# The value half of the first memory's projection computed inside the first cross attention

## The chip, the cores and the metric

One core of a Trainium2 chip runs the whole program. The metric is the device time of one execution in microseconds; the kernel before takes 2530.24 us, the median of three runs (2525.29 to 2534.04). Five engines work beside each other, each with its own queue of instructions in a fixed order: TensorE (PE, with its weight loads shown as PEld), VectorE (DVE), ScalarE (ACT), GpSimd (POOL) and SyncE (SP), which issues most DMAs.

## The reference

Two blocks of layers act on 256 tokens of width 1024. The first block has two layers; each mixes the tokens, then attends to a memory of 256 rows, then applies a feed-forward. The change concerns the first layer: its mixing (a recurrence over time, RWKV, beside a state space part, S5) and the cross attention that follows it:

```python
h = h + y_mix
y_mem = memory_cross_attention(rms_norm(h, norm_xattn), rms_norm(mem, norm_mem), w_q, w_kv, ...)

def memory_cross_attention(h, mem_n, w_q, w_kv, q_gain, k_gain, w_o):
    q = rms_norm((h @ w_q).reshape(b, t, 4, 256), q_gain)
    k, v = split(mem_n @ w_kv, 2)            # w_kv: 1024 x 2048
    k = rms_norm(k.reshape(b, m, 4, 256), k_gain)
    p = softmax(einsum('bthd,bmhd->bhtm', q, k) / 16)
    return einsum('bhtm,bmhd->bthd', p, v) @ w_o
```

The keys and values depend on the memory and the weights alone, and not on the tokens, so they can be computed at any time before they are used. All arithmetic is in 32-bit floats.

## The kernel before

A product with a weight matrix is done in three matmuls. `wt` (L250) loads a weight tile in two halves of 512 KB (128 x 1024 floats) on SP's queue into `raw` buffers; ACT casts each half to a rounded `whi` (L270), DVE subtracts to get the rest `wlo` (L271). `mm3` then multiplies high by high (L320), high by low and low by high (L321, L322). The activations are split in the same way into `xTh` and `xTl` when a norm transposes them (`norm_part`, L379: transposes at L385 on PE, casts at L361 on ACT, subtractions at L362 on DVE, squares at L401 on ACT).

The work is written in phases. `mix0` is the first mixing layer, `xa0` the first cross attention, `ff0` the feed-forward after it. Weight buffers belong to a pool `wp` that is opened anew when a phase wants other sizes: in `mix0` there are 3 raw and 2 split buffers, from `xa0` on 6 and 6 (L47, L48).

Within a phase, pieces of work are Python generators. `drive` (L280) takes one step of each in turn, then one step of a background generator; this order of writing is the priority from which a planner fixes each engine's order when the program is built, by its own costs. In the recurrence, background steps are also tied to stand behind the last matmul of the recurrence written before them (`pace`).

`mem_kv` (L500) computes keys and values of one memory. Its first step loads the memory (two tiles of 512 KB, L506), normalizes it, and allocates `kT` and `v`. Then come four chunks of 512 columns, chunks 0 and 1 keys, 2 and 3 values. A chunk takes two weight tiles (four loads of 512 KB) and eight steps of six matmuls, `psA` group D being its place in PSUM. A key chunk is normalized and transposed afterwards; a value chunk is copied out of PSUM with a scale (L544).

In `mix0` this generator is the background of the recurrence: `rwkv` (L1022) runs `mat` (L1178) for four pairs of heads, two at a time, beside S5 (`s5_main`, L1466, whose scans and products run on DVE and POOL), and takes a step of `mem_kv` per round (L1322). Within `mat`, five rounds of small matmuls (L1225, L1238 to L1241) alternate with a product on DVE (Y, L1227) and a copy on ACT (TZ, L1243); L1248 closes them. After it follow the gate matrix (`s5_glu`) and the output projection.

`xattn` (L576) works on two halves of heads, `attn(0)` and `attn(1)`. Each projects its queries with `w_q` in eight steps of six matmuls (`proj_M`), normalizes and transposes them, and for two blocks of tokens forms scores (L601), softmax and transposed probabilities (L620, L621). Then the product with `v` (L628) and its split follow. The second half starts eight rounds after the first (XI), so its projection lies beside the first half's softmax. `out_proj` with `w_o` is written behind both, and the planner lays its first half beside the second half's softmax. The PSUM group of the query projections alternates between A and D; the product with `v` of the first half uses A (XP).

Of the kernel before, what the change touches and what calls it, by code (L numbers as in the profile page):

```python
# [9 lines left out]
F32 = mybir.dt.float32  # L10
# [22 lines left out]
GC = 3  # L33
RB = 2
XI, XP = 8, ('A', None)
KV_ORD = ((0, 1, 2, 3), (0, 2, 1, 3))
R0 = 2
R1 = 2
# [166 lines left out]
def build(tc, dram, off, out, phases):  # L205
# [7 lines left out]
    ap = None  # L213
# [97 lines left out]
    def idle(n):  # L311
        for _ in range(n):
            yield

    def chain(*fns):
        for f in fns:
            yield from f
# [177 lines left out]
            down_acc(y, lambda k: xh[:, k], lambda k: xl[:, k], name, i, order[0], -1)  # L495
        down_last(y, lambda k: xh[:, k], lambda k: xl[:, k], name, order[last:])

    mem_state, mem_pools, mem_ctx = {}, {}, {}

    def mem_kv(l, tag, st, xp=None):  # L500
        m = [wp.tile([128, 1024], F32, tag="raw", name="mem", bufs=nraw) for _ in range(2)] if rawc == 1024 else None
        if m is None:
            m2 = wp.tile([128, 2, 1024], F32, tag="raw", name="mem", bufs=nraw)
            m = [m2[:, t] for t in range(2)]
        for t in range(2):
            nc.sync.dma_start(m[t], dram("mem")[:, t])  # L506
        xh, xl, rm = norm_T(m, "norm_mem%d" % l, tag, xp)
        gk = ap.tile([128, 2], F32, tag="gk", name="gk", bufs=1)
        V.scalar_tensor_tensor(gk, colr("xa_q_gain%d" % l), 1.0 / 16.0, colr("xa_k_gain%d" % l),
                               op0=ALU.mult, op1=ALU.mult)  # L510
        p = mem_pools[l]
        kT, v = p.tile([128, 8, 256], F32, name="kT"), p.tile([128, 2, 1024], F32, name="v")
        mem_state[l] = (kT, v)
        yield
        def heads_T(c, kn, ks):
            for t in range(2):
                for a in range(2):
                    s = slice(a * 256, a * 256 + 256)
                    V.tensor_scalar(kn[t][:, s], kn[t][:, s], ks[t][:, a:a + 1], None, op0=ALU.mult)
                pt = psC((128, 4, 128))  # L520
                for b in range(4):
                    T.transpose(pt[:, b], kn[t][:, b * 128:(b + 1) * 128], ident)
                for b in range(2):
                    S.activation(kT[:, 4 * c + b:4 * c + 4:2, t * 128:t * 128 + 128], pt[:, b::2], AF.Copy,
                                 scale=gk[:, b:b + 1])

        pend = None
        for c in KV_ORD[l]:
            ps = [psA(tag=tag) for _ in range(2)]
            for j in range(2):  # L530
                w = wt("w_kv%d" % l, 2 * c + j)
                for kk in range(4):
                    k = 4 * j + kk
                    for t in range(2):
                        ts = slice(t * 128, t * 128 + 128)
                        wh, wl = w(kk * 512, 512)
                        mm3(ps[t], xh[:, k, ts], xl[:, k, ts], wh, wl, k == 0, k == 7)
                    yield
                if pend:
                    heads_T(*pend)  # L540
                    pend = None
            if c >= 2:
                for t in range(2):
                    S.activation(v[:, t, (c - 2) * 512:(c - 1) * 512], ps[t], AF.Copy, scale=rm[t])  # L544
                continue
            kn = [st.tile([128, 512], F32, tag="kn", name="kn", bufs=2) for _ in range(2)]
            for t in range(2):
                S.copy(kn[t], ps[t])
            pend = (c, kn, head_norm(kn, rm, 2, 256, st))
        if pend:  # L550
            heads_T(*pend)

    def open_kv(l):
        mem_ctx[l] = ExitStack()
        mem_pools[l] = mem_ctx[l].enter_context(
            tc.tile_pool(name="kv%d" % l, bufs=1, side="right", reuse_waits="tile"))

    def head_norm(src, rm, nh, d, st=None):
        ss = ap.tile([128, 2, nh], F32, tag="hn%d" % nh, name="hn", bufs=2)
# [13 lines left out]
        z = rms_fold(ss, nh, d, EPS, rm)  # L573
        return [z[:, t] for t in range(2)]

    def xattn(l):  # L576
        kT, v = mem_state[l]
        xh, xl, rm = norm_T(ht, "norm_xattn%d" % l)
        oh = ap.tile([128, 8, 256], F32R, tag="oTh", name="oTh", bufs=1)
        ol = ap.tile([128, 8, 256], F32R, tag="oTl", name="oTl", bufs=1)  # L580
        def attn(c):
            ps = yield from proj_M(xh, xl, "w_q%d" % l, c)
            q = ap.tile([128, 2, 512], F32, tag="q", name="q", bufs=2)
            for t in range(2):
                S.copy(q[:, t], ps[t])
            rq = head_norm([q[:, t] for t in range(2)], rm, 2, 256)
            qT = ap.tile([128, 4, 256], F32, tag="qT", name="qT", bufs=2)
            for b2 in range(2):
                pt = psC((128, 2, 2, 128))
                for a in range(2):  # L590
                    for t in range(2):
                        b = 2 * b2 + a
                        T.transpose(pt[:, a, t], q[:, t, b * 128:(b + 1) * 128], ident)
                S.copy(qT[:, 2 * b2:2 * b2 + 2].rearrange("p a t -> p (a t)"), pt.rearrange("p a t c -> p (a t c)"))
            yield
            pT = ap.tile([128, 2, 2, 256], F32, tag="pT", name="pT", bufs=2)
            for t in range(2):
                sc = psB((128, 2, 256))
                for a in range(2):
                    for d in range(2):  # L600
                        T.matmul(sc[:, a], qT[:, 2 * a + d, t * 128:(t + 1) * 128], kT[:, 4 * c + 2 * a + d],  # L601
                                 start=d == 0, stop=d == 1)
                nm = ap.tile([128, 2], F32, tag="nm", name="nm", bufs=2)
                V.tensor_reduce(nm, sc, axis=AX, op=ALU.max, negate=True)
                nb = ap.tile([128, 2], F32, tag="nb", name="nb", bufs=2)
                V.tensor_tensor(nb, nm, rq[t], op=ALU.mult)
                p = ap.tile([128, 2, 256], F32, tag="p", name="p", bufs=2)
                sm = ap.tile([128, 2], F32, tag="sm", name="sm", bufs=2)
                for a in range(2):
                    S.activation(p[:, a], sc[:, a], AF.Exp, bias=nb[:, a:a + 1], scale=rq[t][:, a:a + 1],  # L610
                                 accum_out=sm[:, a:a + 1])
                rc = ap.tile([128, 2], F32, tag="rc", name="rc", bufs=2)
                V.reciprocal(rc, sm)
                for a in range(2):
                    V.tensor_scalar(p[:, a], p[:, a], rc[:, a:a + 1], None, op0=ALU.mult)
                yield
                pt = psC((128, 2, 2, 128))
                for a in range(2):
                    for m in range(2):
                        T.transpose(pt[:, a, m], p[:, a, m * 128:(m + 1) * 128], ident)  # L620
                V.tensor_copy(pT[:, :, :, t * 128:(t + 1) * 128], pt)  # L621
                yield
            for b2 in range(2):
                po = psA((128, 2, 256), XP[c]) if XP[c] else psB((128, 2, 256))
                for a in range(2):
                    b = 2 * b2 + a
                    for m in range(2):
                        T.matmul(po[:, a], v[:, m, c * 512 + b * 128:c * 512 + (b + 1) * 128], pT[:, b // 2, m],  # L628
                                 start=m == 0, stop=m == 1)
                s = slice(4 * c + 2 * b2, 4 * c + 2 * b2 + 2)  # L630
                split(oh[:, s].rearrange("p a t -> p (a t)"), ol[:, s].rearrange("p a t -> p (a t)"),
                      po.rearrange("p a t -> p (a t)"))
                yield

        drive(attn(0), chain(idle(XI), attn(1)))
        out_proj(oh, ol, "w_o%d" % l, LX)

    def diff_attn():
        linit = 0.8 - 0.6 * math.exp(-0.3)
        xh, xl, rm = norm_T(ht, "norm_mix1")  # L640
# [134 lines left out]
            pass  # L775
        tags[0] = "D"
        pace = None
        open_kv(1)
        kv = mem_kv(1, "D", ap, ap)
        next(kv)  # L780
        bg = qkv(1)
# [193 lines left out]
    def mix0():  # L975
        nonlocal junk_at
        with tc.tile_pool(name="z", bufs=1, reuse_waits="tile") as zp:
# [14 lines left out]
                    yield n, ps  # L992

            with tc.tile_pool(name="rw", bufs=1, reuse_waits="tile") as rp:
                open_kv(0)
                zx, s5x = ExitStack(), ExitStack()
                zxp = zx.enter_context(tc.tile_pool(name="zx", bufs=1, side="right", reuse_waits="tile"))
                junk_at = (zxp, 512)
                xh, xl, rm = norm_T(ht, "norm_mix0", xp=zxp)
# [22 lines left out]
    def rwkv(rp, zpair, ya, uT, rrow, s5g):  # L1022
# [62 lines left out]
        zg = zgen()  # L1085
        nonlocal junk_at
        junk_at = (rp, 256)
        kv = mem_kv(0, "D", rp)
        mctx = ExitStack()

        def need(n):
# [29 lines left out]
        st = {}  # L1121
# [639 lines left out]
    for pi, ph in enumerate(phases):  # L1761
# [13 lines left out]
        with tc.tile_pool(name=ph, bufs=1, reuse_waits="tile") as ap:  # L1775
            if ph == "mix0":
                mix0()
            elif ph in ("xa0", "xa1"):
                l = int(ph[2])
                if l not in mem_state:  # L1780
                    open_kv(l)
                    drive(mem_kv(l, "D", ap, ap))
                xattn(l)
                mem_ctx[l].close()
            elif ph == "mix1":
                diff_attn()
# [45 lines left out]
```

## Time and profile before

| | us |
|---|---|
| three timed runs | 2525.29, 2530.24, 2534.04 |
| the profiled execution | 2523.59 |
| its span, first to last instruction | 2521.7 |

The profile is of one execution; 1.9 us of it lie outside the span. A row of the timeline has the start, the duration, the engine, the line of the kernel, the operation, and out<-in by the program's names; x gives how many were merged, and brackets give idle time before it with what ended it. A matmul's end is modelled, so the distance between starts tells what it costs in a stream. PEclk is the granted share of PE's full clock.

### The profile page before, as it was taken

To read this page: it belongs to the slowest core of one execution; us is meant where nothing else is said; L and a number is where in the kernel's file an instruction comes from. 1 tells how busy PE (TensorE), PEld (TensorE's weight loads), DVE (VectorE), ACT (ScalarE), POOL (GpSimd) and SP (SyncE) were. 2 spreads that over 40 slices of the span, in tenths; PEclk is the share of its full clock that TensorE was granted. 3 is DMA by queue.
4 is the path that set the end of the run, shared out by engine and by line. 5 is a ranking of instruction groups with operands and counts; after the bars stand their busy time and mean duration, and the time that the engine had idled before them with its cause. 6 is when DMAs were issued, how large, how long until landed. Compare 5 with 4: busy or idle time off the path is not lost. (4 is left out here: it accounts for less than half of the span.)

```text
span 2521.7 us, 39316 instructions
## 1 busy us (share of the span) xinstructions
PE 2404.3 (95%) x14335; PEld 1997.5 (79%) x14335; DVE 2035.8 (81%) x3506; ACT 1515.2 (60%) x2268; POOL 115.7 (5%) x145
## 2 busy tenths in 40 slices
PE   7888979999999999999999999999998999999999
PEld 6765757999777778787878787877786789976998
DVE  8599665766776679999999999998987778877886
ACT  6322245544665567777777777777766555565554
POOL 2442200000000000000000000000000000000000
PEclk9988979999899989999999999999998999999999
DMA  5311134555444569999999999999994345552553
GB/s 181 109 35 34 52 113 138 190 185 177 154 134 142 192 212 372 345 333 356 362 346 334 357 360 331 359 325 365 348 363 148 118 160 190 186 176 96 182 186 108
DMA packets 154761, 558.19 MB, mean 221 GB/s; under 512 B 17568, under 2 KB 18208, under 8 KB 154560
## 3 DMA queue, kind: packets, MB, share of 16 engines
q1 hardware_dynamic: 152064, 551.62, 62.4%
q10 hardware_dynamic: 2496, 3.99, 0.5%
q8 instruction: 114, 1.87, 0.3%
q14 instruction: 87, 0.71, 0.1%
HBM read 554.50 MB, written 1.05 MB: 220 GB/s over the span
## 5 line engine op out<-in xcount | busy, mean ns | idle before, releaser
L271 DVE TENSOR_TENSOR wlo<-raw,whi 128x1024 fp32r<-128x1024 f32 x1044 | 1253.0, 1226 | 221.3 <-ACT whi L270 207.8
L270 ACT CAST whi<-raw 128x1024 fp32r<-128x1024 f32 x1044 | 1074.7, 1051 | 509.6 <-PE psA L322 213.0
L321 PE MATMUL psB<-wlo,xeh 128*128 128x512 f32 x880 | 351.4, 399 | 3.3 <-DVE wlo L271 3.3
L322 PE MATMUL psB<-whi,xel 128*128 128x512 f32 x880 | 347.6, 395 | 0.0
L320 PE MATMUL psB<-whi,xeh 128*128 128x512 f32 x880 | 345.8, 396 | 0.1
L321 PE MATMUL psB<-xTl,whi 128*128 128x256 f32 x1008 | 283.8, 282 | 0.0
L320 PE MATMUL psB<-xTh,whi 128*128 128x256 f32 x1008 | 281.5, 283 | 1.5 <-DVE fg L1743 1.5
L322 PE MATMUL psB<-xTh,wlo 128*128 128x256 f32 x1008 | 282.6, 281 | 0.0
L321 PEld LDWEIGHTS psB<-wlo,xeh 128*128 128x128 f32 x880 | 165.2, 188 | 47.6 <-DVE wlo L271 9.6
L320 PEld LDWEIGHTS psB<-whi,xeh 128*128 128x128 f32 x880 | 165.2, 188 | 40.0 <-ACT whi L270 1.0
L322 PEld LDWEIGHTS psB<-whi,xel 128*128 128x128 f32 x880 | 165.3, 188 | 38.1
L322 PEld LDWEIGHTS psB<-xTh,wlo 128*128 128x128 f32 x1008 | 191.0, 189 | 0.4
L320 PEld LDWEIGHTS psB<-xTh,whi 128*128 128x128 f32 x1008 | 187.8, 188 | 3.2 <-DVE fg L1743 2.1
L321 PEld LDWEIGHTS psB<-xTl,whi 128*128 128x128 f32 x1008 | 189.4, 188 | 1.1
L321 PE MATMUL psA<-wlo,mhh 128*128 128x512 f32 x448 | 175.8, 394 | 0.2
L320 PE MATMUL psA<-whi,xTh 128*128 128x512 f32 x416 | 170.6, 419 | 5.1 <-ACT whi L270 4.8
L322 PE MATMUL psA<-whi,mhl 128*128 128x512 f32 x448 | 173.8, 392 | 1.2 <-DVE mhl L359 1.2
L321 PE MATMUL psA<-wlo,xTh 128*128 128x512 f32 x416 | 168.7, 409 | 0.1
L322 PE MATMUL psA<-whi,xTl 128*128 128x512 f32 x416 | 163.9, 409 | 0.0
L320 PE MATMUL psA<-whi,mhh 128*128 128x512 f32 x448 | 152.4, 392 | 1.7 <-ACT mhh L358 1.7
L320 PE MATMUL psA<-whi,hh 128*128 128x512 f32 x264 | 103.4, 392 | 1.5 <-ACT hh L358 1.5
L321 PE MATMUL psA<-wlo,hh 128*128 128x512 f32 x264 | 103.2, 391 | 0.0
(568 smaller groups left out, 3901.7 us busy)
## 6 DMA issues: line engine op xcount, KB each, us to landing
raw<-in_w_moe SPq DMA_DIRECT2D x672, 512.0 KB, 6.0
raw<-in_w_bfu SPq DMA_DIRECT2D x88, 512.0 KB, 4.6
raw<-in_w_ffu SPq DMA_DIRECT2D x44, 512.0 KB, 4.5
raw<-in_w_bfd SPq DMA_DIRECT2D x44, 512.0 KB, 4.5
raw<-in_w_kv SPq DMA_DIRECT2D x32, 512.0 KB, 3.6
raw<-in_w_in SPq DMA_DIRECT2D x32, 512.0 KB, 5.7
raw<-in_w_qkv SPq DMA_DIRECT2D x24, 512.0 KB, 4.5
raw<-in_w_ffd SPq DMA_DIRECT2D x22, 512.0 KB, 4.4
```

The costliest lines, as they stand in the source:

```text
L270: S.copy(hi, raw[:, r])
L271: V.tensor_tensor(lo, raw[:, r], hi.bitcast(F32), op=ALU.subtract)
L320: T.matmul(ps, ah, bh, start=st, stop=False)
L321: T.matmul(ps, ah, bl, start=False, stop=False)
L322: T.matmul(ps, al, bh, start=False, stop=sp)
```

## The change

The keys stay in the mixing layer: there `mem_kv` runs with the chunks 0 and 1 alone. Chunks 2 and 3, the values, are computed in `xa0` by a second `mem_kv`, which loads and normalizes the memory again before the query projections are written. Its steps are the background of the two halves of attention, beginning after ten rounds (XK). Before a half takes its product with `v`, the background is run until that half's chunk is done. The query projections of `xa0` use PSUM group A alone, and the values group D. `kT` and `v` have pools of their own, so that `v` is allocated in `xa0`. The second memory is computed as before, with both pools opened together.

```diff
--- before.py
+++ after.py
@@ -33,6 +33,7 @@
 GC = 3
 RB = 2
 XI, XP = 8, ('A', None)
+XK = 10
 KV_ORD = ((0, 1, 2, 3), (0, 2, 1, 3))
 R0 = 2
 R1 = 2
@@ -495,9 +496,9 @@
             down_acc(y, lambda k: xh[:, k], lambda k: xl[:, k], name, i, order[0], -1)
         down_last(y, lambda k: xh[:, k], lambda k: xl[:, k], name, order[last:])
 
-    mem_state, mem_pools, mem_ctx = {}, {}, {}
-
-    def mem_kv(l, tag, st, xp=None):
+    mem_state, mem_ctx, vdone = {}, {}, set()
+
+    def mem_kv(l, tag, st, xp=None, order=None):
         m = [wp.tile([128, 1024], F32, tag="raw", name="mem", bufs=nraw) for _ in range(2)] if rawc == 1024 else None
         if m is None:
             m2 = wp.tile([128, 2, 1024], F32, tag="raw", name="mem", bufs=nraw)
@@ -508,9 +509,7 @@
         gk = ap.tile([128, 2], F32, tag="gk", name="gk", bufs=1)
         V.scalar_tensor_tensor(gk, colr("xa_q_gain%d" % l), 1.0 / 16.0, colr("xa_k_gain%d" % l),
                                op0=ALU.mult, op1=ALU.mult)
-        p = mem_pools[l]
-        kT, v = p.tile([128, 8, 256], F32, name="kT"), p.tile([128, 2, 1024], F32, name="v")
-        mem_state[l] = (kT, v)
+        kT, v = mem_state.get((l, "k")), mem_state.get((l, "v"))
         yield
         def heads_T(c, kn, ks):
             for t in range(2):
@@ -525,7 +524,7 @@
                                  scale=gk[:, b:b + 1])
 
         pend = None
-        for c in KV_ORD[l]:
+        for c in order or KV_ORD[l]:
             ps = [psA(tag=tag) for _ in range(2)]
             for j in range(2):
                 w = wt("w_kv%d" % l, 2 * c + j)
@@ -542,6 +541,7 @@
             if c >= 2:
                 for t in range(2):
                     S.activation(v[:, t, (c - 2) * 512:(c - 1) * 512], ps[t], AF.Copy, scale=rm[t])
+                vdone.add((l, c))
                 continue
             kn = [st.tile([128, 512], F32, tag="kn", name="kn", bufs=2) for _ in range(2)]
             for t in range(2):
@@ -550,10 +550,11 @@
         if pend:
             heads_T(*pend)
 
-    def open_kv(l):
-        mem_ctx[l] = ExitStack()
-        mem_pools[l] = mem_ctx[l].enter_context(
-            tc.tile_pool(name="kv%d" % l, bufs=1, side="right", reuse_waits="tile"))
+    def open_kv(l, part):
+        mem_ctx.setdefault(l, ExitStack())
+        p = mem_ctx[l].enter_context(
+            tc.tile_pool(name="kv%d%s" % (l, part), bufs=1, side="right", reuse_waits="tile"))
+        mem_state[l, part] = p.tile([128, 8, 256] if part == "k" else [128, 2, 1024], F32, name="kT" if part == "k" else "v")
 
     def head_norm(src, rm, nh, d, st=None):
         ss = ap.tile([128, 2, nh], F32, tag="hn%d" % nh, name="hn", bufs=2)
@@ -573,13 +574,13 @@
         z = rms_fold(ss, nh, d, EPS, rm)
         return [z[:, t] for t in range(2)]
 
-    def xattn(l):
-        kT, v = mem_state[l]
+    def xattn(l, kv=None):
+        kT, v = mem_state[l, "k"], mem_state[l, "v"]
         xh, xl, rm = norm_T(ht, "norm_xattn%d" % l)
         oh = ap.tile([128, 8, 256], F32R, tag="oTh", name="oTh", bufs=1)
         ol = ap.tile([128, 8, 256], F32R, tag="oTl", name="oTl", bufs=1)
         def attn(c):
-            ps = yield from proj_M(xh, xl, "w_q%d" % l, c)
+            ps = yield from proj_M(xh, xl, "w_q%d" % l, c, "A" if kv else None)
             q = ap.tile([128, 2, 512], F32, tag="q", name="q", bufs=2)
             for t in range(2):
                 S.copy(q[:, t], ps[t])
@@ -620,6 +621,8 @@
                         T.transpose(pt[:, a, m], p[:, a, m * 128:(m + 1) * 128], ident)
                 V.tensor_copy(pT[:, :, :, t * 128:(t + 1) * 128], pt)
                 yield
+            while (l, 2 + c) not in vdone:
+                next(fill)
             for b2 in range(2):
                 po = psA((128, 2, 256), XP[c]) if XP[c] else psB((128, 2, 256))
                 for a in range(2):
@@ -632,7 +635,11 @@
                       po.rearrange("p a t -> p (a t)"))
                 yield
 
-        drive(attn(0), chain(idle(XI), attn(1)))
+        if kv:
+            next(kv)
+        fill = chain(idle(XK), kv or ())
+        drive(attn(0), chain(idle(XI), attn(1)), bg=fill)
+        drive(fill)
         out_proj(oh, ol, "w_o%d" % l, LX)
 
     def diff_attn():
@@ -775,7 +782,8 @@
             pass
         tags[0] = "D"
         pace = None
-        open_kv(1)
+        open_kv(1, "k")
+        open_kv(1, "v")
         kv = mem_kv(1, "D", ap, ap)
         next(kv)
         bg = qkv(1)
@@ -992,7 +1000,7 @@
                     yield n, ps
 
             with tc.tile_pool(name="rw", bufs=1, reuse_waits="tile") as rp:
-                open_kv(0)
+                open_kv(0, "k")
                 zx, s5x = ExitStack(), ExitStack()
                 zxp = zx.enter_context(tc.tile_pool(name="zx", bufs=1, side="right", reuse_waits="tile"))
                 junk_at = (zxp, 512)
@@ -1085,7 +1093,7 @@
         zg = zgen()
         nonlocal junk_at
         junk_at = (rp, 256)
-        kv = mem_kv(0, "D", rp)
+        kv = mem_kv(0, "D", rp, order=(0, 1))
         mctx = ExitStack()
 
         def need(n):
@@ -1777,10 +1785,15 @@
                 mix0()
             elif ph in ("xa0", "xa1"):
                 l = int(ph[2])
-                if l not in mem_state:
-                    open_kv(l)
+                if (l, "k") not in mem_state:
+                    open_kv(l, "k")
+                    open_kv(l, "v")
                     drive(mem_kv(l, "D", ap, ap))
-                xattn(l)
+                if (l, "v") not in mem_state:
+                    open_kv(l, "v")
+                    xattn(l, mem_kv(l, "D", ap, ap, (2, 3)))
+                else:
+                    xattn(l)
                 mem_ctx[l].close()
             elif ph == "mix1":
                 diff_attn()
```

## Rows read from the trace of the kernel before

**Rows 1.** The page, part 1: busy time, share of the span and instructions of each engine.
```profile
PE 2404.3 (95%) x14335; PEld 1997.5 (79%) x14335; DVE 2035.8 (81%) x3506; ACT 1515.2 (60%) x2268; POOL 115.7 (5%) x145
```

**Rows 2.** Windows: stretch, length, busy us by engine (instructions), PEclk, DMA share, GB/s.
```profile
137.00:237.00 100.00, 84.15 (x912) 58.76 (x912) 91.38 (x228) 25.41 (x60) 34.05 (x31) 0.88 0.11 33
237.00:259.00 22.00, 20.62 (x272) 15.06 (x269) 21.34 (x54) 5.90 (x11) 5.93 (x6) 1.00 0.22 74
259.00:291.00 32.00, 27.70 (x442) 20.18 (x436) 23.93 (x47) 6.43 (x11) 13.00 (x11) 0.95 0.11 34
291.00:314.00 23.00, 23.00 (x419) 18.95 (x418) 8.22 (x19) 8.22 (x17) 0.00 (x0) 1.00 0.23 71
...
367.00:373.00 6.00, 2.22 (x10) 1.45 (x10) 4.84 (x23) 4.53 (x13) 0.00 (x0) 0.75 0.81 229
373.00:386.00 13.00, 12.96 (x48) 9.87 (x48) 11.47 (x16) 8.96 (x12) 0.00 (x0) 0.85 0.92 335
386.00:401.00 15.00, 15.00 (x72) 12.40 (x71) 8.13 (x22) 8.39 (x20) 0.00 (x0) 1.00 0.71 247
401.00:411.00 10.00, 7.71 (x42) 6.22 (x41) 7.75 (x28) 6.99 (x21) 0.00 (x0) 1.00 0.15 54
411.00:429.00 18.00, 17.13 (x81) 14.26 (x80) 9.55 (x17) 6.88 (x13) 0.00 (x0) 1.00 0.33 95
```

**Rows 3.** Timeline (start, us, engine, line), ACT: value copies of chunks 2 and 3.
```profile
279.78 1.39 ACT L544 ACTIVATE v<-psA,rs_y 128x512 f32<-128x512 f32 x2 [0.72 <-PE psA L322]
...
313.27 1.39 ACT L544 ACTIVATE v<-psA,rs_y 128x512 f32<-128x512 f32 x2 [1.86 <-PE psA L322]
```

**Rows 4.** Timeline, all engines, 297 to 300 us: one value step and its neighbours.
```profile
298.02 0.37 ACT L1243 COPY TZ<-psC 128x256 f32<-128x256 f32 x1 [2.09 <-PE psC L1241]
...
298.32 0.50 PE L320 MATMUL psA<-whi,xTh 128*128 128x512 f32 x1
...
299.92 1.09 PE L1248 MATMUL psB<-X,TZ 64*64 64x128 f32 x16
```

**Rows 5.** Timeline, DVE, 251 to 266 us.
```profile
251.64 0.41 DVE L1515 TENSOR_TENSOR R<-M,N 128x256 f32<-128x256 f32 x1
...
253.63 1.21 DVE L271 TENSOR_TENSOR wlo<-raw,whi 128x1024 fp32r<-128x1024 f32 x1
...
256.15 0.43 DVE L1529 SCALAR_TENSOR_TENSOR yab<-y,y 128x256 f32<-128x256 f32 x1 [0.32 <-ACT y L1527]
...
265.37 0.41 DVE L1227 TENSOR_TENSOR Y<-psC,rwc 128x256 f32<-128x256 f32 x1
```

**Rows 6.** Groups by line, 237 to 314 us: count, busy us, mean ns, idle before.
```profile
L271 DVE TENSOR_TENSOR wlo<-raw,whi 128x1024 fp32r<-128x1024 f32 x8 | 10.8, 1351 | 2.4 <-ACT whi L270 2.3
```

**Rows 7.** Timeline, PE, 388 to 390 us: the query projection's matmuls.
```profile
388.21 0.39 PE L320 MATMUL psA<-whi,xTh 128*128 128x512 f32 x1
...
389.38 0.40 PE L322 MATMUL psA<-whi,xTl 128*128 128x512 f32 x1
```

**Rows 8.** Timeline, ACT and PE, 371 to 376 us: the cross attention's start.
```profile
371.60 1.03 ACT L270 CAST whi<-raw 128x1024 fp32r<-128x1024 f32 x1
...
372.69 1.22 PE L320 MATMUL psA<-whi,xTh 128*128 128x512 f32 x2 [1.39 <-ACT whi L270]
...
374.96 0.63 PE L321 MATMUL psA<-wlo,xTh 128*128 128x512 f32 x1
375.39 0.63 PE L322 MATMUL psA<-whi,xTl 128*128 128x512 f32 x1
```

**Rows 9.** Groups by line, 40 to 62 us: the memory's norm.
```profile
L361 ACT ACTIVATE xTh<-psA,cols 128x128 fp32r<-128x128 f32 x12 | 3.9, 359 | 0.2 <-DVE xTl L362 0.2
L362 DVE SCALAR_TENSOR_TENSOR xTl<-psA,cols,xTh 128x128 fp32r<-128x128 f32 x10 | 3.4, 346 | 0.1
L401 ACT ACTIVATE junk<-mem 128x256 f32<-128x256 f32 x8 | 3.3, 410 | 1.1 <-DMA mem<-in_mem 1.0
L385 PE MATMUL psA<-ident,mem 128*128 128x128 f32 x16 | 2.7, 280 | 0.0
```

## The prediction

> **What bounds the kernel now.** I read the page's busy line first: PE is busy for 95% of the span, DVE for 81%, ACT for 60% [rows 1]. The average hides that the change touches two stages with different limits, so the windows by stage come next [rows 2]. In the first mixing layer the value half lies between about 237 and 314 us: the copies of its two chunks out of PSUM stand at 279.78 and 313.27 us [rows 3]. There PE is busy 20.62 of 22, 27.70 of 32 and 23.00 of 23 us, and DVE 21.34 of 22, 23.93 of 32 and 8.22 of 23. So DVE and PE share the limit up to 291 us, and PE alone sets it from 291 to 314. In the first cross attention the value half would go into stretches where PE is busy 12.96 of 13, 15.00 of 15, 7.71 of 10 and 17.13 of 18 us: there PE is the limit throughout, with 2.29 + 0.87 us idle after the projections, and 3.78 us idle at the stage's start (367 to 373). The reader is to see that PE work is taken from one stage that is nearly full and put into one that is full. The sum is thus a difference of two numbers of the same size.
>
> **What is removed from the mixing layer.** Two chunks of 48 matmuls (8 steps of 6 each), 8 casts, 8 subtractions, 4 copies, and 8 weight DMAs of 512 KB on SP's queue, behind which the gate matrix's and the output projection's loads move forward. No transfer is late there, so the DMAs are priced at nothing; PE's idle time in these windows names other waits. The end of the value half doesn't set anything by itself: what counts is how much sooner the recurrence of pairs 2 and 3 ends.
>
> From 291 to 314 us: one step costs PE from 298.32 to 299.92, 1.60 us, and is followed at once by a matmul of the recurrence (L1248) whose input, the copy TZ, was ready at 298.02 + 0.37 = 298.39 [rows 4]. Without the step L1248 starts 1.5 us sooner. There are seven steps here, 11.1 us. In five of them the next instruction's input is ready early in the same way; in the others the copies of the recurrence (0.37 to 0.6 us) come late by part of the step. I take 9 us; bounds 0 and 11.1.
>
> From 237 to 291 us: nine steps, 14.4 us of PE. Here the subtraction wlo stands in DVE's queue among the scans of the state space part: from 251.64 to 265.78 DVE waits only 0.32 us, and the wlo at 253.63 takes 1.21 us of that [rows 5]. Over the whole value half, wlo takes 10.8 us in eight pieces, 1.35 each [rows 6], five of them before 291, so 6.8 us. Where DVE is dense, removing a step gives back its wlo and not its 1.6 us on PE. The bounds are 0 and 14.4; I take 7.5, the DVE's share plus a little, since the PE waits of 4.3 us in 259 to 291 show that PE isn't the only clock there. Sum for the mixing layer: **16.5 us** back (0 to 25.5).
>
> The casts (8 of 1.03 us [rows 8]) and copies (4 of 0.69 [rows 3]) come off an ACT that is busy 20.6 of 77 us: nothing. POOL has no part in the value half.
>
> **What is added to the cross attention.** The same 96 matmuls, in a dense stream: six matmuls apart, 388.21 to 389.38 is 1.17 us for five, 0.234 each [rows 7]. 96 x 0.234 = **22.4 us**. They are laid beside the softmax of each half (the fill starts after ten rounds), but those waits are already covered by the second query projection and the first half of the output projection; what is still open is 2.29 + 0.87 = 3.2 us, of which I let the fill take 2.5 (0 to 6.9 with the idle time at the start). Value copies, casts and subtractions (2.8, 8.2 and 9.7 us) fit on ACT and DVE, which are busy 8.39 and 8.13 of 15 us.
>
> The memory is loaded and normalized a second time. Its work is 16 transposes, 16 casts of 0.359, 16 subtractions of 0.346 and the squares [rows 9]: 5.7 + 3.3 = 9.0 us of ACT, 5.5 of DVE and a short chain, 2.7 of PE. All of it is issued ahead of the query projection: its two loads stand in SP's queue in front of the eight loads of w_q, in two of the six raw buffers. Now the first query matmul starts at 372.69, just after the first cast at 371.60, behind DMAs that move 335 GB/s in 373 to 386 [rows 2, 8]. Two loads ahead of it, 1.05 MB, are 3.1 us at that rate. The ACT and DVE work partly lies in this wait. At best the transposes keep PE awake: today its first matmuls are 0.43 us apart, 374.96 to 375.39, in place of 0.234 [rows 8], and nine of them lose 1.7 us. At worst most of the ACT work stands before the first weights' cast: 10 us. I take **3.5 us** (-1.7 to 10), near the price of the loads, since they can't be avoided.
>
> Two waits are new. The product of probabilities and values of head pair c waits for value chunk 2 + c; behind it in PE's queue stand the splits and the output projection. The query projections of both halves now use PSUM group A alone, so that the second waits for the copies of the first (0.6 us each on ACT). Both waits have value matmuls to run meanwhile, so nothing is added; without that cover it would be 1 to 2 us.
>
> **Sum.** 22.4 + 3.5 - 2.5 = 23.4 us added, 16.5 removed: **+6.9 us**. Against the profiled execution, 2523.59 us, that is 2530.5. That execution lies below all three timed runs, so I put the difference on their median: 2530.24 + 6.9 = **2537 us**. A measurement of this kernel tells about 0.3%, 7.6 us, from no change, so the forecast stands close to that line.
>
> **Rivals.** *They cancel.* PE paces the whole stretch from 237 to 314, and nearly all of the steps comes back (23.5 of 25.5 us), while the cross attention pays the 23.4: 2530. For it: PE is busy 71.3 of 77 us there. Against it: the dense DVE in the first two windows.
>
> *PE time is a plain sum, and faster comes out.* If PE is the only pacing resource in both places, 16 steps of 1.6 us (25.6) leave a stage in which each step pays a gap at both ends, and come back as 22.4 us in a dense stream; and the value matmuls, together with the transposes, also close the 6.9 us that PE idles in the cross attention: -25.6 + 22.4 - 6.9 = -10.1, 2520 us. It decides from the point where the idle time that is closed exceeds 4.4 us with the mixing layer giving everything. For it: idle time of 3.78 us right where the second norm falls. Against it: that idle time waits for loads, and two more are put ahead of them.
>
> *The clock falls.* The value steps fill PE's waits in the mixing layer. The windows show a granted clock of 1.00, 0.95 and 1.00 with them, and 0.88 from 137 to 237 us, where the fill is thinner and PE is busy 84.15 of 100 us [rows 2]. If the stretch from 237 to 314 falls to 0.88, the 45.7 us of PE work left there take 45.7 x (1/0.88 - 1/0.98) = 5.3 us more. With the start of the cross attention at 7 instead of 3.5 us, since the same cold start is met there (0.75 and 0.85 at its edge), the sum is 6.9 + 5.3 + 3.5 = +15.7: 2546. The Trainium skill's page "TensorE: Matmul & The Clock Gate", section "HAM oscillation - how this bites in real kernels", states the rule behind it: a wait between bursts of matmuls puts the gate back to half rate and the next burst starts cold, so work that fills waits is worth more than its own time. By that rule the whole 5.3 us would come; by the rows it is open, because DVE-bound stretches at 1.00 exist too [rows 2].
>
> That the value half is not moved at all I leave out: its weight buffers belong to the pool that opens with the cross attention, so no order of the planner can put it earlier.
>
> **How the numbers follow.** Forecast, with its own range of +2 to +12 us (2532 to 2542): 0.50, of which 0.28 stays within 7.6 us and 0.22 lies over it. Cancel: 0.17, within. Plain sum, faster: 0.13. Clock and cold start: 0.20, slower. So faster 0.13, same 0.45, slower 0.42. The range reaches down to just above the middle of the faster case, 2521, and over the middle of the slow one, 2549; the ends of the unknown terms (25.5 back, 10 at the start) lie outside it only together.
>
> **What would show it.** In the changed kernel's windows the stretch from the second pair of recurrences to the gate matrix should be 13 to 20 us shorter, with wlo gone from it and DVE no longer dense before its end; the gate matrix after it should start some 16 us sooner. The cross attention, from the last matmul of the mixing layer to the first of the feed-forward, should grow by about 23 us, its first query matmul coming some 3 us later than now, and PE dense from there on. I am wrong if the mixing layer gives back under 10 or over 22 us, if value matmuls leave PE idle for more than 3 us beside the softmax, or if the first query matmul comes over 7 us later. A granted clock under 0.9 where it is now 0.95 or more speaks for the third rival.

## The result and the profile after

The changed kernel takes 2545.79 us, the median of seven runs (2541.07 to 2557.54), beside 2526.34 us for the kernel before (2523.55 to 2534.04); the ratio is 1.0083, 95% interval 1.0069 to 1.0097. By that ratio it is 21 us slower. I forecast 6.9 us slower, with a range up to 2549: the side was right, the size was a third. The profiled execution took 2552.4 us (span 2550.6); 23.1 of the 28.8 us that it has over the profiled execution of the kernel before lie in the two stages that the change touches, the rest behind them.

The page's busy line, to be read against [rows 1], has more work on PE and hardly less on DVE:

```profile
PE 2416.8 (95%) x14351; PEld 2010.0 (79%) x14351; DVE 2040.5 (80%) x3537; ACT 1521.4 (60%) x2292; POOL 114.0 (4%) x145
```

The two stages are measured by the last matmuls of their output projections. The next two fences show one group by tile each for the kernel before and the changed one: count, shortest, median and longest duration in ns, first and last start in us. `mh` is the mixing layer's output projection, `oTh` the cross attention's.

```profile
L320 PE MATMUL psA<-whi,mh x32: 389/399/499, 341.9 to 366.3; 128*128 128x512 f32 x32
...
L320 PE MATMUL psA<-whi,oTh x32: 389/389/582, 411.3 to 440.9; 128*128 128x512 f32 x32
```

```profile
L321 PE MATMUL psA<-whi,mh x32: 392/394/497, 341.2 to 365.6; 128*128 128x512 f32 x32
...
L321 PE MATMUL psA<-whi,oTh x32: 389/391/580, 437.4 to 464.0; 128*128 128x512 f32 x32
```

From these four lines the whole result can be read. The mixing layer ends 366.3 - 365.6 = 0.7 us sooner, where 16.5 were forecast and anything under 10 was named as a sign of being wrong. From its end to the end of the cross attention it is 98.4 us instead of 74.6: 23.8 us more, where 23.4 were forecast.

The windows of the changed kernel, with the columns of [rows 2]:

```profile
237.00:259.00 22.00, 12.06 (x80) 6.82 (x79) 18.31 (x48) 4.33 (x13) 5.92 (x6) 0.69 0.07 25
259.00:291.00 32.00, 22.94 (x362) 17.34 (x362) 21.88 (x47) 2.61 (x5) 12.08 (x11) 0.68 0.01 2
291.00:314.00 23.00, 21.44 (x602) 19.39 (x602) 5.38 (x16) 5.55 (x13) 1.22 (x2) 0.93 0.01 3
...
373.00:386.00 13.00, 10.03 (x30) 7.64 (x31) 10.63 (x28) 9.69 (x20) 0.00 (x0) 0.74 0.75 254
386.00:401.00 15.00, 15.00 (x74) 12.23 (x73) 10.79 (x30) 11.95 (x27) 0.00 (x0) 1.00 0.76 268
401.00:411.00 10.00, 10.00 (x48) 8.43 (x47) 6.42 (x15) 5.20 (x11) 0.00 (x0) 1.00 0.53 168
411.00:429.00 18.00, 18.00 (x88) 15.05 (x87) 10.68 (x25) 10.46 (x21) 0.00 (x0) 1.00 0.54 170
429.00:442.00 13.00, 13.00 (x60) 10.91 (x59) 6.56 (x13) 6.42 (x14) 0.00 (x0) 1.00 0.26 84
442.00:465.00 23.00, 23.00 (x112) 19.07 (x111) 11.85 (x17) 10.82 (x20) 0.00 (x0) 1.00 0.34 113
```

Below 291 us PE is now idle for 9.94 + 9.06 = 19 us, at a granted clock of 0.69 and 0.68 instead of 1.00 and 0.95; in 291 to 314 it has 602 matmuls to do instead of 419: the recurrence has been left behind. Between 260 and 277 us the granted clock is at the lower of its two levels, 1.2 of 2.4 GHz, and PE is busy for 13.37 of the 17 us:

```profile
260.00:277.00 17.00, 13.37 (x169) 10.39 (x170) 11.06 (x24) 0.86 (x2) 5.89 (x6) 0.50 0.01 1
```

From 386 us on the cross attention is dense and at full clock.

What PE waits for between 237 and 314 us (us in total, times, longest), first in the kernel before, then in the changed one:

```profile
PE psA L1518 <- DVE R L1515: 3.2, 4, 1.4
PE psC L1238 <- DVE Y L1227: 2.5, 1, 2.5
```

```profile
PE psA L1526 <- DVE R L1523: 12.2, 3, 5.6
PE psC L1246 <- DVE Y L1235: 3.4, 2, 2.6
PE psA L1488 <- DVE rs_in L349: 3.0, 1, 3.0
PE psC L521 <- DVE kn L518: 1.1, 1, 1.1
PE psC L1233 <- ACT TZ L1251: 0.6, 2, 0.4
```

R is the state of the state space part, and L1526 its output matmul. The reader is to see that the PE time set free went into waits of PE, nearly all of them on DVE: 20.3 us instead of 5.7. They run the other way too: in the same stretch POOL waits 12.8 us in the changed kernel to write the next R until PE has read the last one (`POOL R L1497 <- PE psA L1526`), a wait that the kernel before doesn't have. The timeline shows what stands behind such a wait. Here is PE around 252 us in the changed kernel (start, duration; in brackets the idle time before and its releaser):

```profile
249.68 1.06 PE L1526 MATMUL psA<-R,s5c 128*32 128x256 f32 x2
...
251.89 1.94 PE L521 MATMUL psC<-ident,kn 128*128 128x128 f32 x8 [1.15 <-DVE kn L518]
253.75 1.92 PE L1526 MATMUL psA<-R,s5c 128*32 128x256 f32 x4
255.60 0.91 PE L1201 MATMUL psC<-rwc,TZ 64*64 64x64 f32 x12
```

L1201 is the recurrence of a later pair; its counterpart in the kernel before starts at 236.63 us:

```profile
236.63 0.56 PE L1193 MATMUL psC<-rwc,TZ 64*64 64x64 f32 x10
```

It stands 19 us later, behind the state space matmuls and the eight transposes L521 of the last key chunk. The wait for the chunk's norm is only 1.15 us of PE's idle time here; the longest, ahead of the state space matmuls at 248.82 us, is 5.6. In the kernel before, the tail of a key chunk was written after four steps of the next chunk. In the changed one the last key chunk has no next, and its tail is written at once, while DVE still computes its norm.

### The profile page after: what moved, and what is told of

Its sections match the earlier page's. It is cut to its first block, busy times and chain, and to the rows that moved or that the text cites. A ratio compares the mean times of both kernels' runs of the same rounds, so it can differ in the third digit from the quotient of the medians.

```text
span 2550.6 us, 39403 instructions
## 1 busy us (share of the span) xinstructions
PE 2416.8 (95%) x14351; PEld 2010.0 (79%) x14351; DVE 2040.5 (80%) x3537; ACT 1521.4 (60%) x2292; POOL 114.0 (4%) x145
```

## The experiments

Three readings stood against each other: the *order* (PE's fixed order has been laid otherwise, and ready matmuls stand behind waiting ones), the *clock* (my third rival), and the *state space chain* (DVE and POOL pace the stage whatever PE does). Layer ends are those of the `mh` group in the profiled execution.

**The key tail four steps later.**

```
+        if order == (0, 1):
+            yield from idle(4)
         if pend:
             heads_T(*pend)
```

> The changed kernel, with the tail of the last key chunk (its scaling and eight transposes) written four background steps later, as the kernel before had it. Order theory: in the changed kernel these transposes stand early in PE's order, wait for DVE's head norm, and hold the recurrence of pairs 2 and 3 behind them (its first matmuls at 255.6 instead of 236.6 us); so the mixing layer, whose last matmul ends at 366.0 us, ends 8 to 16 us sooner (350 to 358), and the kernel takes 2530 to 2538. Clock theory (PE without the value steps falls to half clock and works more slowly through the same list): the layer ends within 3 us of 366, the granted clock of 237 to 291 stays at 0.7. State space theory (the chain through DVE and POOL with single buffers paces the stage): within 3 us of 366, clock as it comes.

Measured: 2536.23 us (2533.37 to 2542.65, ratio 1.0044, 1.0031 to 1.0056); the layer's last group starts at 357.9 instead of 365.6, 7.7 us sooner, just under what the order theory asked and far over the 3 us of the others:

```profile
L321 PE MATMUL psA<-whi,mh x32: 388/396/499, 333.5 to 357.9; 128*128 128x512 f32 x32
```

The edit moves more than the tail, since all of PE's order is laid anew: the recurrence now starts at 239.97 us instead of 255.60, and the granted clock of 237 to 314 us rises from 0.76 to 0.84. How much of the 7.7 us is the clock's is not shown. And the waits for R are still there (12.6 us):

```profile
260.82 0.28 PE L1248 MATMUL psC<-TZ,rwc 64*64 64x64 f32 x4
267.12 1.06 PE L1528 MATMUL psA<-R,s5c 128*32 128x256 f32 x2 [6.02 <-DVE R L1525]
268.12 0.47 PE L1249 MATMUL psC<-Y,TZ 64*64 64x64 f32 x2
```

PE stops in the middle of a block of the recurrence for 6.02 us, and the rest of that block (L1249, whose first half had run by 261 us) runs as soon as L1528 is through. The Trainium skill, page "PSUM — Partial Sum Buffer", section "Engine vs sequencer instructions", says that matmuls start and complete in program order; this row agrees: matmuls that were ready stood behind a wait of 6.02 us.

**Filler in place of the value steps**, behind which the key tail comes as before (first kernel), or with the tail ahead (second).

```
+        if order == (0, 1):
+            for n in range(4):
+                ps = [psA(tag=tag) for _ in range(2)] if n % 2 == 0 else ps
+                for k in range(4):
+                    for t in range(2):
...
+                        mm3(ps[t], xh[:, k, ts], xl[:, k, ts], wh, wl, ...)
+                    yield
```

> The changed kernel, with 16 steps of six matmuls (128x512, the memory against the last key chunk's weights, result not used) put back where the value steps stood; the key tail comes after the first four, so PE's order is that of the kernel before; no weights are loaded, cast or subtracted for them. Clock theory: the granted clock of 237 to 291 returns to 0.95 or more, and in spite of 22 us more of PE work the mixing layer ends no later than 366, at about 359 (the 6.8 us of wlo that DVE no longer has). Order theory: also about 359, since the order is mended, but later than the run with the late tail alone by what the matmuls cost (8 to 15 us). State space theory: 364 to 368, wherever the clock is.

> The same 16 steps of filler, but behind the early key tail, so that PE's order ahead of them is that of the changed kernel. Clock theory: as with the late tail, about 359, clock 0.95 or more. Order theory: the wait for the head norm is still there, and the matmuls come on top: 370 to 385. State space theory: 364 to 368.

Measured: 2551.02 us (1.0102, 1.0087 to 1.0116), layer's last group at 371.6; and 2551.08 us (1.0098, 1.0081 to 1.0114), at 370.0. The layer's last group and the windows of the second:

```profile
L321 PE MATMUL psA<-whi,mh x32: 389/394/500, 345.7 to 370.0; 128*128 128x512 f32 x32
```

```profile
237.00:259.00 22.00, 16.89 (x90) 10.64 (x88) 19.09 (x50) 3.25 (x8) 6.67 (x7) 0.65 0.00 1
259.00:291.00 32.00, 30.42 (x526) 22.77 (x526) 20.12 (x46) 3.34 (x6) 11.71 (x10) 0.98 0.01 2
291.00:314.00 23.00, 23.00 (x461) 19.21 (x458) 3.37 (x11) 4.44 (x10) 0.00 (x0) 1.00 0.01 2
```

The clock theory asked for 359 with the clock restored. It was restored in part (1.00 and 0.84 up to 291 us in the first kernel, here 0.65 up to 259 us and 0.98 and 1.00 from there on), and the layer got longer, not shorter. Against the changed kernel the 22.5 us of filler (96 matmuls at the forecast's 0.234) cost 370.0 - 365.6 = 4.4 us: in this order PE's work is almost free. That doesn't hold for every order: in the first kernel, against the late tail alone, they cost 371.6 - 357.9 = 13.7 us, inside the 8 to 15 that the order theory gave for it. Nor does either kernel price the clock, since filler brings work and clock at once. The state space theory's 364 to 368 was missed by both. The order theory's number for the second kernel held at its lower edge, its 359 for the first did not. That 359 rested on the 6.8 us of DVE's wlo, and here is the last step of the state space part (L1529, then L1548) in the kernel before and in the first filler kernel, which has no wlo:

```profile
L1529 DVE SCALAR_TENSOR_TENSOR yab<-y,y x4: 420/426/427, 173.7 to 293.0; 128x256 f32<-128x256 f32 x4
```

```profile
L1548 DVE SCALAR_TENSOR_TENSOR yab<-y,y x4: 415/421/426, 174.7 to 293.2; 128x256 f32<-128x256 f32 x4
```

293.0 and 293.2: DVE's freed time brought the state space part nothing (in the changed kernel, without the value half's wlo too, the step comes at 296.8). I had also taken PE's order as restored; it was only the tail's place. Counted in the traces, 494 of the recurrence's matmuls (those of 64x64 tiles) start after the last output matmul of the state space part in the kernel before, 662 in the changed one, 582 with the late tail and 628 in the first filler kernel.

**Two buffers for R, M and N** (NR and NM from 1 to 2).

> The changed kernel, with two buffers instead of one for the state space part's three work tiles (R, M and N). State space theory: the mixing layer ends 6 us or more sooner (by 360), since DVE and POOL no longer wait for each other's tiles. Order and clock theories: within 3 us of 366; the transposes of the key tail still run at about 252 us, and the clock stays at 0.7.

Measured: 2549.76 us (1.0098, 1.0083 to 1.0113), the layer's last group at 368.6, 3.0 us later. Waits of PE in 237 to 314 us:

```profile
PE psA L1526 <- DVE R L1523: 14.4, 2, 8.0
PE psC L1246 <- DVE Y L1235: 5.7, 2, 5.3
```

The state space theory's gain isn't there, and 3.0 us later is the edge of what the others allowed. With two buffers POOL no longer waits for PE to read R, but PE's waits for R grew, and the last output matmul of the state space part starts at 297.6 us instead of 294.0. That the planner counts on R sooner and lays its matmuls further ahead is my reading; no run separates it.

**State space steps in every third, then every fourth round** (SE from 2 to 3, to 4, both with the late tail), **and every third in the kernel before.**

> The run with the late key tail, and the steps of the state space part written in every third round of the mixing layer instead of every second. Planned-order theory (without the value steps the planner, by its own costs, puts the state space part's output matmuls ahead of recurrence matmuls, and PE then waits for their input R: 12.2 us of waits in the changed kernel between 237 and 314 us and 12.6 us with the late tail, 3.2 before; 245 recurrence matmuls are left behind the last of them with the late tail, 288 in the changed kernel, about 90 before): here only 46 are left behind it, the waits for R fall under 6 us, and the mixing layer ends 4 to 9 us sooner than with the late tail (349 to 354 us, against 358.3). State space theory (the chain through DVE and POOL sets the end, whatever the order): writing it later makes it end later than 294 us, and the layer ends at 360 or later. Clock theory: no change beyond 3 us unless the granted clock of 237 to 291 rises above 0.9.

> The same with the state space steps in every fourth round. Planned-order theory: about as with every third round, within 4 us, since as few recurrence matmuls stand behind the last output (47); if the state space part now ends too late, up to 5 us later. State space theory: later again than with every third round, by 5 us or more.

> The kernel before (value half in the mixing layer) with the state space steps in every third round, as a control. Planned-order theory: its order was sound already (3.2 us of waits for R), so there is little to gain: within 4 us of 2525.8. If writing the state space part later is good in itself, whatever the value steps do, it gains as much here as with the late tail (4 to 9 us).

Measured: 2539.59 us (1.0059, 1.0045 to 1.0072), last group at 356.2; 2534.93 us (1.0037, 1.0023 to 1.0051), at 358.0; and the control 2528.79 us (1.0007, 0.9998 to 1.0016), last group at 366.2, within the 4 us that the order theory allowed. With every third round it asked for 349 to 354: missed, with 1.7 us won in the layer and none at the end of the cross attention (456.1, with the late tail 455.9). With every fourth round the layer ends within the 4 us of the third that the order theory allowed, and not 5 us later as the state space theory asked. The counts of recurrence matmuls in these expectations are not those of the traces: there 176 of the recurrence's matmuls stand behind the last output with every third round and none with every fourth, and the count doesn't foretell the waits. The state space theory's "360 or later" was missed as well. The waits of PE with every third round:

```profile
PE psA L1528 <- DVE R L1525: 8.4, 3, 4.1
PE psC L1279 <- DVE ST L1273: 5.4, 1, 5.4
```

The wait for R goes from 12.6 to 8.4 us, and 5.4 us appear for ST, whose DVE instruction now stands among the scans. The recurrence's matrices end 10 us sooner (294.4 instead of 304.7) and its tail gives most of it back. With every fourth round the waits for R are 14.2 us. Moving the state space part in the order moves the wait; it doesn't remove it.

**Memory read two rounds into the query projection** (no `next(kv)` ahead, XK from 10 to 2, with the late tail).

> The run with the late key tail, and the second reading and norm of the memory no longer ahead of the query projection but begun two rounds into it. My term of 3.5 us for the start of the cross attention: the first query matmul comes 3 to 4 us sooner after the end of the mixing layer (6.0 us behind it as in the kernel before, instead of 9.5), and the stage's end moves by as much, 2 to 4 us. Rival (the memory's loads, casts and transposes cost the same wherever they stand, and in the dense stretch they delay the weights): the first query matmul is sooner, but the last matmul of the output projection comes within 1.5 us of where it was, counted from the end of the mixing layer (98.2 us).

Measured: 2535.14 us (1.0039, 1.0025 to 1.0052). The first query matmul starts 5.9 us behind the layer's last group instead of 9.9, 4.0 sooner as the first part said, and the last group of the stage comes 454.5 - 356.4 = 98.1 us behind the layer's, where it was 455.9 - 357.9 = 98.0. The rival is right: the second reading of the memory costs the same wherever it stands.

**No wait for R** (with the late tail).

```
-                        T.matmul(py[...], cc[:, i, gp], R[:, x, i].rearrange("p c t -> p (c t)"),
+                        T.matmul(py[...], cc[:, i, gp], uT[:, j],
```

> The run with the late key tail; the state space part's output matmuls read its input u instead of R (so its output leaves out the state; all scans and products on DVE and POOL are still done), and PE never waits for R. If these waits (12.6 us between 237 and 314 us with the late tail) are what keeps the mixing layer from giving back what the value steps cost on PE, the layer ends 8 to 13 us sooner than 358.3, at 345 to 350. If DVE's own work paces the recurrence (its copies of Y and ST stand in DVE's queue among the scans), the PE waits go over to Y and ST, and the layer ends within 4 us of 358.3.

Measured: 2529.81 us (1.0021, 1.0010 to 1.0031). The output projection and the largest waits of PE in 237 to 314 us:

```profile
L321 PE MATMUL psA<-whi,mh x32: 390/398/494, 324.1 to 348.4; 128*128 128x512 f32 x32
```

```profile
PE psC L1122 <- DVE ct L1304: 6.8, 2, 3.9
PE psC L1248 <- DVE Y L1237: 5.5, 3, 3.2
PE psC L521 <- DVE Y L1237: 4.3, 1, 4.3
```

The layer ends 9.5 us sooner than with the late tail, inside 345 to 350, at the same granted clock (0.83 over 237 to 314 us, with the late tail 0.84). With all of DVE's and POOL's work still there, PE's dependence on R was worth that; part of the waits came back as waits for Y. The run takes away more than PE's waits, though: DVE and POOL no longer wait for PE to have read R either, and the order is laid anew. The last step of the state space part, with the late tail and here:

```profile
L1539 DVE SCALAR_TENSOR_TENSOR yab<-y,y x4: 418/424/426, 177.0 to 294.4; 128x256 f32<-128x256 f32 x4
```

```profile
L1539 DVE SCALAR_TENSOR_TENSOR yab<-y,y x4: 415/418/424, 171.3 to 277.1; 128x256 f32<-128x256 f32 x4
```

It comes 17.3 us sooner, so PE and the state space chain had held each other up; which side of that was worth how much is not shown. Late tail and no waits together end the layer 365.6 - 348.4 = 17.2 us sooner, 17.9 before that of the kernel before.

**The last value steps of the kernel before, four or five rounds later.** Four steps (then six) go among the recurrence's last matmuls.

```
-              bg=chain(every_n(zrest(), ZN), kv), slow=slow, every=SE)
+              bg=chain(every_n(zrest(), ZN), held(28), idle(4), kv), slow=slow, every=SE)
```

Here `held(n)` gives n steps of kv; the second kernel has `held(26), idle(5)`.

> The kernel before, with the last four value steps (6.4 us of PE) written four rounds later, so that three of them stand among the last matmuls of the recurrence, where PE waits 7.3 us for ct between 306 and 345 us. If value work is only free in waits that nothing else covers, the mixing layer ends 3 to 6 us sooner (361 to 364 instead of 366.7), the granted clock of 314 to 342 rises from 0.63, and the kernel takes 2520 to 2523, faster than both. Rival (the weights' loads and the casts for them hold the next stage's, or the tail is bound by its chain through DVE and ACT, whose start does not move): within 2 us of before.

> The same with the last six value steps (9.6 us) written five rounds later. By the first reading the recurrence ends sooner by another 1.5 to 3 us, but more work stands in the tail than it has waits (7.3 us): from 2 us sooner to 2 us later than with four steps. By the rival: within 2 us of before, or later.

Measured: 2518.86 us (2516.25 to 2527.83), ratio to the kernel before 0.9979, 0.9968 to 0.9990: faster than both kernels, 5 us under the one before. The layer's last group starts at 364.0 instead of 366.3: 2.3 us, short of the 3 us expected. The other 3 us of the total stand behind the two stages, and no run shows that the edit is their cause. The layer's last group; then the wait for ct in 306 to 345 us and the window of 314 to 342, each in the kernel before and here:

```profile
L320 PE MATMUL psA<-whi,mh x32: 389/399/503, 339.7 to 364.0; 128*128 128x512 f32 x32
```

```profile
PE psC L1112 <- DVE ct L1294: 7.3, 2, 4.4
```

```profile
PE psC L1112 <- DVE ct L1294: 4.2, 2, 3.6
```

```profile
314.00:342.00 28.00, 18.92 (x159) 15.36 (x158) 17.18 (x61) 9.86 (x20) 0.00 (x0) 0.63 0.06 20
```

```profile
314.00:342.00 28.00, 20.36 (x109) 16.29 (x107) 18.14 (x57) 12.12 (x22) 0.00 (x0) 0.82 0.12 40
```

The wait is 4.2 us where it was 7.3, and the granted clock 0.82 where it was 0.63. With six steps the last group starts sooner still (362.6), but the kernel takes 2528.30 us (1.0011, 1.0001 to 1.0020). What its 3.7 us were lost to stands behind both stages and stays open.

## Why the prediction was right in its side and wrong in its size

**The cross attention: right, by its parts.** Forecast 23.4, measured 23.8. The first query matmul starts 375.46 - 365.6 = 9.9 us behind the layer's last group, before 372.69 - 366.3 = 6.4 [rows 8]: the 3.5 us that I took. From there to the last group it is 88.5 us instead of 68.2: 20.3, against 22.4 - 2.5 = 19.9. From its first matmul on PE idles 0.6 us up to 386 us and not at all behind it, as the test at the end of the prediction asked. That the 3.5 us "can't be avoided" is borne out by the run with the memory read late.

**The mixing layer: wrong.** The step that failed is "Without the step L1248 starts 1.5 us sooner", and with it the 9 and 7.5 us summed from such steps. It takes one instruction out and leaves the others where they stood. But PE's order is laid anew when the program is built: the last key tail moved ahead (shown: 7.7 us of the layer when put back), and state space matmuls moved ahead of the recurrence while their input came no sooner (shown: waits for R from 3.2 to 12.2 us, and 9.5 us of the layer when the dependence on R is taken away). The two are 17.2 us, about what I had expected to get back; but the second run also takes away the 3.2 us that the kernel before waits, and shortens the state space chain itself, so that the sums agree is not a proof that 16.5 us was the right measure of PE's work. I knew of the planner, but asked only whether the moved matmuls would fit where they go, not what would move into the place that they leave.

**The DVE share, 6.8 us of wlo: wrong.** I read "dense" from 14 us of DVE's queue [rows 5]. The state space part ended at 293.0 with wlo and 293.2 without. An engine that is busy over a stretch is not for that reason what paces the chain that runs through it. Which step does pace it stays open: two buffers didn't shorten it, and without PE's reading of R it ended 17.3 us sooner.

**The total: inside the range by luck.** The side came from the cross attention alone. That 2546 us lies inside the range up to 2549 is owed to the range's width and not to the sum, which had the layer wrong by 15.8 us.

**The rivals.** "The clock falls" came closest in number (2546), by chance: it has 11.2 us given back and 26.9 added, where 0.7 and 23.8 were measured. Its sign was seen: 0.69 and 0.68. Its price stays open. PE was busy for 13.37 us at half the clock between 260 and 277 us, so there alone up to 6.7 us could be the clock's (an estimate, half of that time); but filler that brought part of the clock back made the layer longer, and the 9.5 us without R came at the same clock. The Trainium skill's page "TensorE: Matmul & The Clock Gate", section "HAM oscillation — how this bites in real kernels", which I cited there, agrees as far as the clock was low where PE waited; that filling the waits is worth more than the work's own time, no run here showed (22.5 us of filler cost 4.4; the four late steps, 6.4 us of work, won 2.3). "They cancel" and "plain sum" both needed the layer to give back 23 us or more; with both waits gone it gave 17.9.

## What to carry to other kernels

Before pricing a removal, ask what the planner will put into the place: look for instructions on the same engine whose inputs come from a slow chain, and for tails that were written behind the work that goes. A stage that shows PE busy for 93% need not give back PE work that is taken out of it: here 25.6 us came out and 0.7 came back, while the same work cost 23.8 us in a dense stage. If anything is moved, move it into a wait that nothing covers, as the four value steps in the recurrence's tail, which won 2.3 us of the layer.

## What the runs showed that I had not expected

The same instructions far behind the change take different times in the profiled executions of different kernels. Around 1990 us, at the end of an attention that no kernel here changes, a stretch ran at 1.2 GHz for 10.2 us in the kernel before and for 20.5 us in the run with six late value steps; the windows around it:

```profile
1986.00:2007.00 21.00, 19.69 (x87) 14.07 (x88) 15.24 (x46) 10.71 (x35) 0.00 (x0) 0.76 0.09 32
```

```profile
1982.00:2005.00 23.00, 22.16 (x74) 14.66 (x73) 13.83 (x39) 9.28 (x31) 0.00 (x0) 0.55 0.05 17
```

In these profiled executions the second kernel was 4.6 us ahead before this place and 0.5 us behind after it. Why is open; the run with four late value steps, the fastest of all, had 20.5 us at 1.2 GHz there too. A gain of 3 us in one stage is therefore read from that stage's own rows, and from many runs, before it is read from the total.
